# Layer 0's gates: the order of the squares of the weights, and the distance of the adaLN sums

## The chip, the core and the metric

One NeuronCore of a Trainium2 chip runs the whole program. Its engines work side by side: TensorE (PE: matmuls, with the weight loads shown as PEld), VectorE (DVE), ScalarE (ACT), GpSimd (POOL), and SyncE (SP), which here only issues DMAs. Each engine takes its own instructions strictly in order, and waits on semaphores for the others. The metric is the time of one execution on the device in microseconds (us); the kernel before has a median of 1865.01 us in three runs (1864.7 to 1866.88).

## What is computed

A stack of two layers over 1024 latent tokens and 256 context tokens of width 1024. Each layer modulates its input by adaLN, mixes tokens, multiplies with a SiLU gate, projects out and normalises.

```python
def adaln(cvec, w, b):
    m = jax.nn.silu(cvec) @ w + b
    return jnp.split(m, 3, axis=-1)
...
        shift, scale, gate = adaln(c, ada_w[i], ada_b[i])
        shift_c, scale_c, gate_c = adaln(c_ctx, ada_w[i], ada_b[i])
        h = x * (1.0 + scale[:, None, :]) + shift[:, None, :]
        h_c = ctx * (1.0 + scale_c) + shift_c
...
        q_lat, kv_lat, k_pe, gate = jnp.split(t @ w_in, splits, axis=-1)
        q = (rms_norm(q_lat, g_qa) @ w_qb).reshape(bsz, n, A_HEADS, A_NOPE + A_ROPE)
        kv = (rms_norm(kv_lat, g_kva) @ w_kvb).reshape(bsz, n, A_HEADS, A_NOPE + A_V)
```

Layer 0 is multi-head latent attention (the last lines), layer 1 differential attention. This document is about a stretch of layer 0: the columns of `t @ w_in` that make the gate, and what is done beside them.

## The kernel before

**The gates.** For 1280 tokens in 10 tiles of 128 and 1024 gate columns in 4 quarters of 256 there are 40 gate tiles. `gate_tile` (L310) is 24 matmuls in a row (8 slices of the width, three products of high and low halves each), then a SiLU on ScalarE and a store of the result. The first two are done at the end of the stage before; the other 38 in the loop under `with spool("p0g")`. The weights of the next quarter are loaded and split by `gate_w` (L297): ScalarE casts the high half, GpSimd subtracts the low half.

**What runs beside them.** After each of these 38 tiles the loop calls `next(side, None)` once, so the generator `beside_gates` gives 38 stretches of other work. Only TensorE's order is written by hand (`manual_schedule`): its instructions run exactly in the order of the program text, so a matmul that is issued in a stretch stands between two gate tiles. On the other engines and in SP's queue a scheduler puts instructions in an order of its own before the run, by when it takes them to be ready and by their place in the text; after that their order is fixed too. A tile of a tag with a few buffers can be written when an earlier user of that buffer is done.

**The first part of the side work**, `up_weights` (L372), prepares layer 0's up-projection weights and the scales for its half-precision attention. It has a tag `u` with four buffers, through which all loads go. Its items, each followed by a `yield`:

- `q_weight`, four times: load 128 x 768 of w_qb, multiply by a gain on VectorE (L382), cast the high half on ScalarE (L176), subtract the low half on GpSimd (L177).
- `k_weight`, two times: the same for 128 x 512 of w_kv (L291).
- `rope_chunk`, three times: load a chunk of the rotary keys; for the two latent chunks load cosines and sines as well and rotate (`rope`, L277 to L280, with a fourth buffer of `u`); for the context chunk copy.
- `square`, ten times: ScalarE squares a chunk of weights into a tile `wsq` (three buffers); the first two (`sq_v`, L392) load their chunk of the value weights into `u` first, the next two square the k weights, the last six the q weights. Each `square` from the third on also issues the `column_sums` of the square two before: one matmul (L403) into a bank `c`, of which there are two, and VectorE's maximum of it (L407), after which the bank is free.

Then follow the last two column sums, the range of the rotary keys, one small matmul (L448), the scales, and the store of the split keys to `kpf_d` (L459, L460).

**The second part**, `ada_dve` (L463), makes three thirds of adaLN's product, (layer 1 shift), (layer 1 scale) and (layer 0 gate), for the two conditioning vectors s = 0, 1. Per third it loads eight tiles `adw` of 128 x 1024 (three buffers) and sums them on VectorE, weighted by a column `ck`, into `acc[0]` and `acc[1]` (three buffers): L497 begins a sum, L501 adds to it. `finish` then sums over partitions: for a shift or scale 8 matmuls for each vector (L470) and one addition (L473); for the gate two matmuls for each vector (L482), two additions (L483) and a store to `gates_d` (L484). The steps of `finish` are taken, one in a stretch, while the next third is being summed.

Behind the gates come the first projections and loads for layer 0's attention; SP's loads for them (L290, L621, L622, L627) stand behind the last `gates_d` store in its queue.

Of the kernel before, what the change touches and what calls it, by code (L numbers as in the profile page):

```python
# [14 lines left out]
ALU = mybir.AluOpType  # L15
AX = mybir.AxisListType

P = 128
D = 1024
# [34 lines left out]
def hybrid_kernel(  # L54
# [7 lines left out]
    pe, act, dve, pool, sp = nc.tensor, nc.scalar, nc.vector, nc.gpsimd, nc.sync  # L62
# [6 lines left out]
    def nm(s):  # L69
        uid[0] += 1  # L70
        return f"{s}_{uid[0]}"
# [39 lines left out]
    def col(n, name, dt=F32):  # L111
        return cpool.tile([P, n], dt, tag=name, name=name)
# [11 lines left out]
    sc = col(16, "sc")  # L124
# [82 lines left out]
    acc = [hs.tile([P, D], F32, name=f"hacc{s}") for s in range(2)]  # L207
# [12 lines left out]
    for k in range(KT):  # L220
        for g in (1, 0):
            w = hs.tile([P, D], F32, tag="adaw", bufs=6, name=nm("adaw"))
# [149 lines left out]
    def up_weights(pa):  # L372

        u = lambda w=768: pa.tile([P, 768], F32, tag="u", bufs=4, name=nm("u"))[:, :w]
        vm = pa.tile([P, 8], F32, name="vm")
        kr = pa.tile([ROPE, NTOK], F32, name="kr")

        def q_weight(j, hh):
            c = slice(hh * 768, hh * 768 + 768)
            ws = u()  # L380
            sp.dma_start(ws, w_qb[j * P:(j + 1) * P, c])
            dve.tensor_scalar_mul(ws, ws, gqa[:, j:j + 1])  # L382
            split(wqH[:, j, c], wqL[:, j, c], ws, e_lo=pool)

        def k_weight(hh):
            c = slice(hh * 512, hh * 512 + 512)
            kv_weight(c, wkH[:, c], wkL[:, c], u(512))

        def sq_v(dst, c):
            wv = u(512)  # L390
            sp.dma_start(wv, w_kv[:, 1024 + c.start:1024 + c.stop])
            act.activation(dst, wv, AF.Square, scale=gkva)  # L392

        norms = ((0, [sq_v], 1024), (1, [lambda d_, c: act.activation(d_, fv(wkH[:, c]), AF.Square)], 1024),
                 (2, [lambda d_, c, j=j: act.activation(d_, fv(wqH[:, j, c]), AF.Square) for j in range(2)], 1536))
        jobs = [(f, i, c0, j == 0, j == len(parts) - 1) for i, parts, n in norms
                for c0 in range(0, n, 512) for j, f in enumerate(parts)]
        cur = [None]

        def column_sums(sq, i, c0, first, stop):  # L400
            if first:
                cur[0] = bank("c")
            pe.matmul(cur[0], onr, sq, start=first, stop=stop)  # L403
            if stop:
                dst = vm[:, i:i + 1]
                d_ = vm[:, 6:7] if c0 else dst
                dve.tensor_reduce(d_, cur[0], axis=AX.X, op=ALU.max)  # L407
                if c0:
                    dve.tensor_tensor(dst, dst, d_, op=ALU.max)

        def rope_chunk(c0, n):
            c = slice(c0, c0 + n)
            kt = u(512)[:ROPE]
            sp.dma_start(kt[:, :n], kp_d[:, c])
            if c0 < SEQ:
                tabs = [u(512)[:ROPE] for _ in range(2)]
                for j in range(2):
                    sp.dma_start(tabs[j], cs0[j, :ROPE, c])
                rope(kt, n, tabs[0], tabs[1], u(512)[:ROPE], kr[:, c])
            else:  # L420
                dve.tensor_copy(kr[:, c], kt[:, :n])

        wait = []

        def square(f, i, c0, first, stop):
            sq = pa.tile([P, 512], F32R, tag="wsq", bufs=3, name=nm("wsq"))
            f(sq, slice(c0, c0 + 512))
            wait.append((sq, i, c0, first, stop))
            if len(wait) == 3:
                column_sums(*wait.pop(0))  # L430

        sq = [(square, a) for a in jobs]
        rc = [(rope_chunk, a) for a in CHUNKS]
        for f, a in (sq[:2] + [(q_weight, (j, hh)) for j in range(2) for hh in range(2)] + [(k_weight, (hh,)) for hh in range(2)]
                     + [rc[0], sq[2], rc[1], sq[3], rc[2]] + sq[4:]):
            f(*a)
            yield
        for w in wait:
            column_sums(*w)
            yield  # L440
        dve.tensor_reduce(vm[:ROPE, 3:4], kr, axis=AX.X, op=ALU.max, apply_absolute_value=True)
        for i, n in ((0, KVL), (1, KVL), (2, 4 * QL)):
            pool.tensor_scalar(vm[:, i:i + 1], vm[:, i:i + 1], 1.01 * n, 1e-30, op0=ALU.mult, op1=ALU.add)
        pool.tensor_tensor(vm[:, 0:3], vm[:, 0:3], poshalf[:, 0:1].to_broadcast([P, 3]), op=ALU.pow)
        yield
        yield
        bk = bank("c")
        pe.matmul(bk[:, :ROPE], vm[:ROPE, 3:4].to_broadcast([ROPE, P]), idn[:ROPE, :ROPE], start=True, stop=True)  # L448
        dve.tensor_reduce(vm[:, 4:5], bk[:, :ROPE], axis=AX.X, op=ALU.max)
        dve.tensor_tensor(vm[:, 1:2], vm[:, 1:2], vm[:, 4:5], op=ALU.max)  # L450
        p2 = pa.tile([P, 3, 2], F32, name="p2")
        pow2_of(vsc0, usc0, vm[:, 0:1], 8192.0, p2[:, 0, :])
        pow2_of(ksc0, vm[:, 4:5], vm[:, 1:2], 32.0, p2[:, 1, :])
        pow2_of(qsc0, vm[:, 5:6], vm[:, 2:3], 32.0, p2[:, 2, :])
        dve.scalar_tensor_tensor(esc0, vm[:, 4:5], SC0, vm[:, 5:6], op0=ALU.mult, op1=ALU.mult)
        dve.scalar_tensor_tensor(sh0, ksc0, math.log(4.0) / SC0, qsc0, op0=ALU.mult, op1=ALU.mult)
        kh_, kl_ = (u().bitcast(F16)[:ROPE, :NTOK] for _ in range(2))
        split16(kh_, kl_, kr, ksc0[:ROPE, :])
        sp.dma_start(kpf_d[:, 0, :], kh_)  # L459
        sp.dma_start(kpf_d[:, 1, :], kl_)  # L460
        yield

    def ada_dve(tile_, thirds):  # L463

        def finish(layer, g, acc):
            if g < 2:
                cb = bank("c")
                for s, a_ in enumerate(acc):
                    for j in range(KT):
                        pe.matmul(cb[:, 2 * j + s:2 * j + s + 1], a_[:, j * P:(j + 1) * P], ones[:, 0:1],  # L470
                                  start=True, stop=True)
                    yield
                dve.tensor_tensor(cols1[:, g * KT:g * KT + KT, :], cb[:, :16].rearrange("p (a b) -> p a b", b=2),  # L473
                                  adac[:, g * KT:g * KT + KT].rearrange("p (a o) -> p a o", o=1).to_broadcast([P, KT, 2]),
                                  op=ALU.add)
                return
            gr = tile_("adw")[:1, :]
            sp.dma_start(gr, ada_b[layer:layer + 1, g * D:(g + 1) * D])
            for s, a_ in enumerate(acc):
                for c0 in (0, 512):  # L480
                    bk = bank("c")
                    pe.matmul(bk[:1, :512], ones[:, 0:1], a_[:, c0:c0 + 512], start=True, stop=True)  # L482
                    dve.tensor_tensor(a_[:1, c0:c0 + 512], gr[:, c0:c0 + 512], bk[:1, :512], op=ALU.add)  # L483
                sp.dma_start(gates_d[layer, s:s + 1, :], a_[:1, :])  # L484
                yield

        end = iter(())
        for layer, g in thirds:
            acc = []
            for k in range(KT):  # L490
                w = tile_("adw")
                sp.dma_start(w, ada_w[layer, k * P:(k + 1) * P, g * D:(g + 1) * D])
                for s in range(2):
                    ck = sc[:, 2 * k + s:2 * k + s + 1]
                    if k == 0:
                        acc.append(tile_("acc"))
                        dve.tensor_scalar_mul(acc[s], w, ck)  # L497
                        if s == 0:
                            next(end, None)
                    else:  # L500
                        dve.scalar_tensor_tensor(acc[s], w, ck, acc[s], op0=ALU.mult, op1=ALU.add)  # L501
                if k:
                    next(end, None)
                yield
            end = finish(layer, g, acc)
        yield
        for _ in end:
            yield
# [31 lines left out]
    def beside_gates():  # L540
        with spool("p0side") as sp_:
            for i, _ in enumerate(up_weights(sp_)):
                if i % 5 in (1, 4):
                    yield
        with spool("p0side2") as sp_:
            t_ = lambda tag: sp_.tile([P, D], F32, tag=tag, bufs=3, name=nm(tag))
            yield from ada_dve(t_, ((1, 0), (1, 1), (0, 2)))
# [358 lines left out]
    with ow_ctx, spool("o0") as op0:  # L906
# [14 lines left out]
        for t in (8, 9, 0, 1, 2, 3, 4, 5, 6, 7):  # L921
# [5 lines left out]
            s = 0 if t < 8 else 1  # L927
# [574 lines left out]
```

## Time and profile before

| | us |
|---|---|
| median of three runs | 1865.01 |
| the profiled execution | 1863.27 |
| its span (first to last instruction) | 1861.5 |
| TensorE busy in the span | 1688.1 (91%) |
| VectorE, ScalarE, GpSimd busy | 1239.5, 1076.3, 834.9 |
| first gate tile starts, last one ends | 97.4, 244.5 |

A row of a timeline reads: start, duration, engine, line, operation, out<-in, shape, count; in brackets the engine's idle time before it and who ended it. A row of waits reads: engine, what waited, who released it, then total us, times, longest. A row of stretches has the stretch, its length, TensorE's busy time and number of matmuls, the granted share of its clock, the busy share of the DMA engines and what they moved. A row of SP gives the issue of a DMA, not its landing. Rows with a count above one are merged: their duration runs from the first start to the last end.

### The profile page before, as it was taken

The numbers are of one execution on the slowest core, as the hardware profiler recorded it, in microseconds if no ns is written. First come the engines' busy times: TensorE is split into PE (matmuls) and PEld (weight loads), VectorE is DVE, ScalarE is ACT, GpSimd is POOL, SyncE is SP. The second block draws the span as 40 slices with busy tenths as digits, with TensorE's granted clock in tenths as the row PEclk, the third lists the DMA queues.
The fourth block names the chain that finished last, engine by engine and source line by source line (L and its number), as shares of the span: only waits on it lengthen the run. The fifth ranks groups of instructions, "written<-read, shape, count | busy, mean of one in ns | idle before, by whom it ended". The sixth has DMA issues, their size and how long they took to land. (4 is left out here: it accounts for less than half of the span.)

```text
span 1861.5 us, 36543 instructions
## 1 busy us (share of the span) xinstructions
PE 1688.1 (91%) x14468; PEld 1232.8 (66%) x14468; DVE 1239.5 (67%) x2069; ACT 1076.3 (58%) x2143; POOL 834.9 (45%) x741
## 2 busy tenths in 40 slices
PE   7889988999999998969879899999999999988998
PEld 3888965666666565557656575767676666666776
DVE  7547655665565666526764777777877777878674
ACT  3442156877877778811123676676767676767542
POOL 1443026767767776846652213232222222423654
PEclk8998999999999999979989999999999999999999
DMA  8247530111110113153334222222211212223342
GB/s 297 73 119 217 166 107 14 42 32 37 39 45 24 39 43 79 50 172 128 124 118 115 70 66 58 61 65 63 64 50 41 48 48 58 65 52 139 100 132 68
DMA packets 111225, 154.84 MB, mean 83 GB/s; under 512 B 13415, under 2 KB 84679, under 8 KB 111054
## 3 DMA queue, kind: packets, MB, share of 16 engines
q1 hardware_dynamic: 104238, 146.22, 26.5%
q10 hardware_dynamic: 6816, 6.29, 1.0%
q8 instruction: 114, 1.87, 0.4%
q14 instruction: 57, 0.47, 0.1%
HBM read 98.65 MB, written 27.07 MB: 68 GB/s over the span
## 5 line engine op out<-in xcount | busy, mean ns | idle before, releaser
L733 POOL TENSOR_TENSOR pl<-p,ph 128x1024 f16<-128x1024 f32 (+1 forms) x176 | 363.8, 2073 | 152.5 <-ACT ph L732 124.9
L1187 ACT ACTIVATE p<-ps_b,mx 128x512 f32<-128x512 f32 (+1 forms) x384 | 230.3, 617 | 82.0 <-DVE mx L1183 81.8
L731 ACT ACTIVATE p<-ps_a,esc 128x1024 f32<-128x1024 f32 (+1 forms) x176 | 189.0, 1074 | 99.5 <-PE ps_a L789 93.6
L713 DVE TENSOR_REDUCE mx<-ps_a 128x1 f32<-128x1024 f32 x128 | 155.5, 1222 | 135.3 <-PE ps_a L711 135.2
L732 ACT CAST ph<-p 128x1024 f16<-128x1024 f32 (+1 forms) x176 | 177.1, 1006 | 5.5
L1181 DVE TENSOR_REDUCE mx<-ps_b 128x1 f32<-128x512 f32 x256 | 165.5, 681 | 0.0
L802 PE MATMUL ps_d<-Vh,pl 128*128 128x65 f16 x1344 | 147.0, 194 | 6.7 <-POOL pl L733 6.7
L799 PE MATMUL ps_d<-Vh,ph 128*128 128x65 f16 x1344 | 149.1, 195 | 0.0
L801 PE MATMUL ps_d<-Vl,ph 128*128 128x64 f16 x1344 | 147.9, 193 | 0.0
L185 PE MATMUL ps_b<-h1H,wH 128*128 128x512 f16 (+1 forms) x384 | 133.5, 348 | 14.1 <-DVE pl L182 7.1
L185 PE MATMUL ps_b<-wH,h1H 128*128 128x256 f16 x512 | 139.5, 272 | 4.4 <-ACT p L1187 4.1
L1212 POOL TENSOR_TENSOR sm<-sm,us 128x1 f32<-128x1 f32 x64 | 19.5, 305 | 271.2 <-DVE sm L1191 257.9
L187 PE MATMUL ps_b<-wH,h1L 128*128 128x256 f16 x512 | 139.5, 273 | 0.0
L186 PE MATMUL ps_b<-wL,h1H 128*128 128x256 f16 x512 | 139.5, 273 | 0.0
L1164 PE MATMUL ps_b<-KS,QS 128*128 128x512 f16 (+1 forms) x384 | 126.1, 345 | 11.6 <-DVE pl L182 6.1
L799 PEld LDWEIGHTS <-ph 128*128 128x128 f16 x1344 | 123.8, 98 | 18.1 <-issue 4.9
L187 PE MATMUL ps_b<-h1H,wL 128*128 128x512 f16 (+1 forms) x384 | 133.0, 346 | 0.8 <-DVE wL L182 0.8
L186 PE MATMUL ps_b<-h1L,wH 128*128 128x512 f16 (+1 forms) x384 | 133.1, 347 | 0.0
L801 PEld LDWEIGHTS <-ph 128*128 128x128 f16 x1344 | 124.5, 99 | 12.2 <-issue 0.3
L787 PE MATMUL ps_a<-qH,KH 100*128 100x512 f16 x320 | 122.4, 383 | 9.7 <-ACT p L731 4.5
L1165 PE MATMUL ps_b<-KS,Q 128*128 128x512 f16 (+1 forms) x384 | 129.2, 345 | 0.0
L802 PEld LDWEIGHTS <-pl 128*128 128x128 f16 x1344 | 123.7, 98 | 8.3 <-POOL pl L733 8.3
(369 smaller groups left out, 5138.5 us busy)
## 6 DMA issues: line engine op xcount, KB each, us to landing
ws<-in_dw SPq DMA_DIRECT2D x30, 512.0 KB, 3.9
adw<-in_ada_w SPq DMA_DIRECT2D x24, 512.0 KB, 4.4
g<-sg_d SPq DMA_DIRECT2D x18, 512.0 KB, 3.5
adaw<-in_ada_w SPq DMA_DIRECT2D x16, 512.0 KB, 6.8
sg_d<-gg ACTq DMA_DIRECT2D x40, 128.0 KB, 4.7
o<-o_d SPq DMA_DIRECT2D x10, 512.0 KB, 3.6
o_d<-op SPq DMA_DIRECT2D x7, 640.0 KB, 3.7
xt<-in_xT SPq DMA_DIRECT2D x16, 256.0 KB, 3.6
```

What stands on the lines that cost most here:

```text
L185: pe.matmul(ps, aH, bH, start=start, stop=False, skip_group_check=skip)
L186: pe.matmul(ps, aH, bL, start=False, stop=False, skip_group_check=skip)
L187: pe.matmul(ps, aL, bH, start=False, stop=stop, skip_group_check=skip)
L713: dve.tensor_reduce(mx[:, t, 0:1], ps, axis=AX.X, op=ALU.max)
L731: act.activation(p32[:, :n], st, AF.Exp, scale=esc0)
L732: act.copy(ph[:, :n], p32[:, :n])
L733: pool.tensor_tensor(pl[:, :n], p32[:, :n], ph[:, :n], op=ALU.subtract)
L799: pe.matmul(pv[:, t, :], ph[:, ts], Vh[:, k, h, :], start=(k == kcs[0] and t == 0), stop=False, skip_group_check=True)
L801: pe.matmul(pv[:, t, :V0], ph[:, ts], Vl[:, k, h, :], start=False, stop=False, skip_group_check=True)
L802: pe.matmul(pv[:, t, :], pl[:, ts], Vh[:, k, h, :], start=False, stop=(k == NT - 1), skip_group_check=True)
L1181: dve.tensor_reduce(mx[:, 2 + 2 * m + i:3 + 2 * m + i], b, axis=AX.X, op=ALU.max, negate=True)
L1187: act.activation(p[m][:, c0:c0 + n], b, AF.Exp, bias=nb, accum_out=sm[:, 2 + 3 * m + i:3 + 3 * m + i])
```

## The change

Edits in the two generators and in their caller. `CHUNKS` has three entries.

```diff
-        for f, a in (sq[:2] + [(q_weight, (j, hh)) for j in range(2) for hh in range(2)] + [(k_weight, (hh,)) for hh in range(2)]
-                     + [rc[0], sq[2], rc[1], sq[3], rc[2]] + sq[4:]):
+        for f, a in [(q_weight, (j, hh)) for j in range(2) for hh in range(2)] + [(k_weight, (hh,)) for hh in range(2)] + rc + sq:
             f(*a)
             yield
...
+        def add(k, s):
+            ck = sc[:, 2 * k + s:2 * k + s + 1]
+            if k == 0:
+                acc.append(tile_("acc"))
+                dve.tensor_scalar_mul(acc[s], ws[k], ck)
+            else:
+                dve.scalar_tensor_tensor(acc[s], ws[k], ck, acc[s], op0=ALU.mult, op1=ALU.add)
+
         for layer, g in thirds:
-            acc = []
+            acc, ws = [], []
             for k in range(KT):
-                w = tile_("adw")
-                sp.dma_start(w, ada_w[layer, k * P:(k + 1) * P, g * D:(g + 1) * D])
-                for s in range(2):
-                    ck = sc[:, 2 * k + s:2 * k + s + 1]
-                    if k == 0:
-                        acc.append(tile_("acc"))
-                        dve.tensor_scalar_mul(acc[s], w, ck)
-                        if s == 0:
-                            next(end, None)
-                    else:
-                        dve.scalar_tensor_tensor(acc[s], w, ck, acc[s], op0=ALU.mult, op1=ALU.add)
-                if k:
+                ws.append(tile_("adw"))
+                sp.dma_start(ws[k], ada_w[layer, k * P:(k + 1) * P, g * D:(g + 1) * D])
+                if k == 0:
+                    continue
+                if k == 1:
+                    add(0, 0)
+                    add(1, 0)
+                    yield
                     next(end, None)
-                yield
+                    add(0, 1)
+                    add(1, 1)
+                    yield
+                else:
+                    next(end, None)
+                    add(k, 0)
+                    add(k, 1)
+                    yield
             end = finish(layer, g, acc)
...
             for i, _ in enumerate(up_weights(sp_)):
-                if i % 5 in (1, 4):
+                if (i % 2 if i < 12 else i % 3 == 2):
                     yield
```

- The items of `up_weights` now run: four q weights, two k weights, three rotary chunks, ten squares. Before, two squares came first and two stood between the rotary chunks.
- The caller asks for two items in each of the first six stretches and for three in each of the next four; before it asked for two and three in turn. The part fills ten stretches, where it filled nine and a part of the tenth.
- A third of adaLN still fills eight stretches. Its tiles 0 and 1 are loaded in the first of them and summed for vector 0 there, for vector 1 in the second; `finish` of the third before takes its first step in the second stretch (it was the first) and its second in the third. All thirds begin one stretch later, so the first step of `finish` stands two gate tiles later than before, and so does the second; the last third's two steps stand one gate tile later.
- No instruction is added or taken away.

## The prediction

> **What bounds the kernel now.** I read the page first, then the waits of TensorE inside the gates of layer 0 (97 to 245 us), then TensorE's busy time and clock by stretch, then the engines' timelines around the two places found.
>
> ```profile
> span 1861.5 us, 36543 instructions
> ```
> ```profile
> PE ps_c L470 <- DVE acc L501: 4.4, 1, 4.4
> PE ps_c L403 <- DVE vm L407: 3.2, 1, 3.2
> PE ps_c L403 <- ACT wkH L176: 3.0, 1, 3.0
> ```
> ```profile
> core 0: us, PE busy (x), PEclk, DMA share, GB/s
> 121.90:125.80 3.90, 0.52 (x2) 1.00 0.36 98
> 125.80:132.70 6.90, 4.04 (x18) 0.51 0.28 77
> 132.70:167.20 34.50, 34.50 (x281) 1.00 0.65 192
> 167.20:170.20 3.00, 0.12 (x2) 1.00 0.96 265
> 170.20:180.40 10.20, 8.64 (x40) 0.50 0.84 230
> ```
>
> In this stage TensorE is full except at two places, both inside small matmuls that were threaded between gate tiles: column sums of squares (L403) and the last step of an adaLN third (L470). Since TensorE's order is written by hand, whatever is late there stops all gate tiles behind it. Idle time is only part of the price: after each place the clock stands at half.
>
> Place one: idle 3.90 - 0.52 = 3.4 and 6.90 - 4.04 = 2.9, and half of the 4.04 us worked at clock 0.51, 2.0: together **8.3 us**. Place two: 2.9 and 1.6 idle, and half of 8.64, 4.3: **8.8 us**. A full-clock matmul costs 34.5/281 = 0.123 us, so a gate tile of 24 takes 2.9 us.
>
> Why place one is late: both waits are for VectorE in the end.
>
> ```profile
> 114.32 0.62 DVE L382 TENSOR_SCALAR u<-u,gqa 128x768 f32<-128x768 f32 x1 [11.23 <-DMA u<-in_w_qb]
> ...
> 116.35 1.82 DVE L382 TENSOR_SCALAR u<-u,gqa 128x768 f32<-128x768 f32 x1 [0.39 <-DMA u<-in_w_qb]
> ...
> 124.15 0.68 DVE L407 TENSOR_REDUCE vm<-ps_c 128x1 f32<-128x512 f32 x1
> 126.63 0.01 DVE L277 LOAD_MASK_SELECT u<-u  x1 [1.79 <-POOL wkL L177]
> 126.63 0.71 DVE L277 STREAM_SHUFFLE u<-u 32x512 f32<-32x512 f32 x1
> 127.25 0.66 DVE L278 TENSOR_TENSOR kr<-u,u 32x512 f32<-32x512 f32 x1
> 127.84 0.67 DVE L407 TENSOR_REDUCE vm<-ps_c 128x1 f32<-128x512 f32 x1
> ...
> 131.10 0.67 DVE L278 TENSOR_TENSOR kr<-u,u 32x512 f32<-32x512 f32 x1
> ```
>
> The reductions L407, which free the two banks "c", sit in VectorE's queue behind weight scalings and a rotation (L277) that wait for buffers. The third column sum finds its bank at 124.8 instead of 122, the fourth at 128.5.
>
> **The change: squares last.** Item by item, the old order put the first column sum (cs0) after the fourth tile of this loop; the new one asks two items per tile, so cs0 is issued with item 11, in the sixth call: two tiles later.
>
> ```profile
> 115.60 0.39 PE L403 MATMUL ps_c<-wsq,onr 128*128 128x512 f32 x1
> ...
> 171.76 0.58 PE L470 MATMUL ps_c<-ones,acc 128*128 128x1 f32 x2 [4.43 <-DVE acc L501]
> ```
>
> TensorE therefore reaches cs0 at 115.6 + 2 x 2.9 = 121.4. But cs0 needs the square of the first value-weight chunk, and that chunk is loaded into a buffer of the tag u, of which there are four. Before, its load was the first of all:
>
> ```profile
> 107.04 0.91 SPq L391 DMA_DIRECT2D u<-in_w_kv  x2
> 108.00 6.54 SPq L381 DMA_DIRECT2D u<-in_w_qb  x4
> 117.77 2.46 SPq L290 DMA_DIRECT2D u<-in_w_kv  x2
> ```
> ```profile
> 111.07 0.72 ACT L392 ACTIVATE wsq<-u,gkva 128x512 fp32r<-128x512 f32 x1 [3.53 <-DMA u<-in_w_kv]
> ```
> ```profile
> 115.89 8.05 POOL L177 TENSOR_TENSOR wqL<-u,wqH 128x768 fp32r<-128x768 f32 x4 [9.30 <-ACT wqH L176]
> 123.91 2.67 POOL L177 TENSOR_TENSOR wkL<-u,wkH 128x512 fp32r<-128x512 f32 x2
> ```
> ```profile
> DMA to landing us min/median/max: 1.9/3.0/6.8
> ```
> (the last row is that of all loads into u.) Now it is the sixteenth user of u, behind four q weights, two k weights, eight tiles of two rotations and one of a copy. It gets the buffer that held the second rotation's cosines. The chain to it:
>
> - First q weight: issued at 107.0, landed 4.0 later like the first load before (111.07), so 111.1. From VectorE's scaling to GpSimd's subtraction 115.89 - 114.32 = 1.6: GpSimd starts at 112.7 instead of 115.9.
> - GpSimd's six subtractions are back to back, 8.05 + 2.67 = 10.7 long. I add 1.4 for a hole: the second q weight lands about 113, while GpSimd is in its first subtraction, and a scaling in that state took 1.82 us, not 0.62. Then comes its cast, so the second subtraction begins near 115.9, not 114.5. The first rotation's last buffer is free at 124.8, against 126.6 before.
> - From there to the end of the second cosine multiply: 131.77 - 126.63 = 5.1 before, with two reductions in between that are gone; what is left is 1.3 for shuffle and multiply, 2.0 for the reload (the least landing is 1.9) and 1.3 again: 129.4.
> - SP issues the copy's load, 0.4, then the value chunk; 3.0 to land, 0.75 to square: TensorE goes on at **133.6**.
>
> So TensorE stands 133.6 - 121.4 = 12.2 us where it stood 6.3 before. The idle time ends at half clock; I take the 2.0 us that place one cost so far. At the fourth column sum the bank of the second must be reduced first, 0.8 (a 0.67 us reduction and its two handovers; VectorE is free now). The other six sums have a gate tile for each three of them and wait for nothing. New price 15.0, old 8.3: **+6.7 us**. The ten squares and their ten matmuls are the same in number and cost.
>
> Bounds: without the hole -1.4; if loads land as late as 6.8 (row above) the q weights arrive together, without a hole but from 113.8 on, +1.3; the value chunk in 4.0 instead of 3.0, +1.0; half clock for 3.3 us of work instead of 4.0 (second row below), -0.35, or for 8.64 as at place two, +2.3; the bank 0 to 1.2.
>
> ```profile
> 49.90:53.00 3.10, 0.01 (x1) 1.00 0.00 2
> 54.20:57.50 3.30, 3.30 (x11) 0.50 0.10 23
> ```
>
> [...] The row shows a scaling that is slow beside GpSimd, not why. [...]
>
> **adaLN sums.** The first third's sums are now consumed two tiles later on TensorE for one vector and again one tile on for the other (L470 after the tenth and eleventh tile behind the L448 matmul instead of the eighth and ninth). The loads do not move against the work they hang on: the new loop begins one call later, but its DMAs and sums are free of TensorE's order and follow the store of kpf_d, as before.
>
> ```profile
> 152.31 1.42 DVE L497 TENSOR_SCALAR acc<-adw,sc 128x1024 f32<-128x1024 f32 x2 [4.20 <-DMA adw<-in_ada_w]
> 154.87 18.49 DVE L501 SCALAR_TENSOR_TENSOR acc<-adw,sc,acc 128x1024 f32<-128x1024 f32 x14 [1.14 <-DMA adw<-in_ada_w]
> ```
> ```profile
> 168.11 7.65 POOL L177 TENSOR_TENSOR wgL<-wgs,wgH 128x256 fp32r<-128x256 f32 x6 [22.29 <-ACT wgH L176]
> ```
>
> TensorE was 4.4 us early; two tiles are 5.8, so 1.4 to spare and no wait: **-8.8 us**. Against it, a bound: if VectorE keeps the written order, the second sum waits for tile 1 (154.87), and tile 0 is free only after 154.87 + 1.3 + 0.7 = 156.8, not 153.7.
>
> ```profile
> adw<-in_ada_w SPq DMA_DIRECT2D x24, 512.0 KB, 4.4
> ```
>
> Its buffer's next load then lands at 161.2, where the fifth of the 14 sums began at 154.87 + 4 x 1.2 = 159.7: 1.6 late, 0.2 short of the spare time. GpSimd's splits (168.11) stretch the last sums as before. So 0 to 3 us can come back, 0 is nearest. The same 16 sums and 32 L470 matmuls per third remain. Later thirds have their two tiles more as well.
>
> **The end of the stage.** The last gate row is stored one tile later, and SP's loads for the attention queue behind it.
>
> ```profile
> 239.46 0.22 SPq L484 DMA_DIRECT2D gates_d<-acc  x1
> 239.78 0.83 SPq L290 DMA_DIRECT2D p<-in_w_kv  x2
> ```
> ```profile
> 250.38 0.87 DVE L291 TENSOR_SCALAR p<-p,gkva 128x512 f32<-128x512 f32 x2
> ```
>
> They move by a tile, from 239.8 to 242.7; at 3 us to land (the median above), one behind the other, they are there by about 248, and VectorE asks at 250.4: that cover holds. Without it, up to 1 us.
>
> **Sum:** +6.7 - 8.8 + 0 = -2.1 us. The profiled execution took 1863.27 us (span and 1.8 around it), 1.7 less than the median of the runs, 1865.01. So 1861.2 in its terms, **1862.9** for the median. By all bounds at once it is -4.7 to +6.9 us; 0.2% is 3.7 us, and less than that can't be told from no change.
>
> **Rivals.** (1) *The first wait is short*: GpSimd's chain has no hole, half clock lasts 3.3 us, the bank is free in time: -1.4 - 0.35 - 0.8 against my sum, so -4.65, 1860.4. For it: one q scaling at 0.62 us while loads landed 1 us apart. Against: four q loads now share the burst. (2) *It does what it says*, both waits vanish, -17.1 us, 1847.9: needs the value chunk by 121.4, so a buffer of u by about 117.6; the third row of SP shows a buffer of the first q weight free only at 117.8 and the next in line taking it. (3) **Slower:** the sums of the first third still come late at L470, over some 2 us, and the clock halves again there. Price 3 of wait and 4.3 of half clock as at place two: -2.1 + 7.3 = +5.2, 1870.2. It decides from about 2 us of lateness, which takes the written order and one slow load. For it: 3.1 us of idle time at 49.90 were followed by half clock. Against: 1.4 us to spare.
>
> [...]
>
> **How the numbers follow.** Forecast 0.50 (its own range 1861.3 to 1867), rival 1 0.24, rival 2 0.08, rival 3 0.18. Faster is 1 and 2, 0.32; slower is 3. The range 1858.8 to 1869.2 leaves out rival 2 and half of rival 3.
>
> **What would show it.** Right: one wait of about 12 us at L403 for the value chunk (its load issued near 129.8), none over 1 us at another L403, none at L470, the clock at half once instead of twice in the stage, L448 some 6 to 7 us later than 143.7 and the last gate tile ending within 3 us of 244.5. Wrong: cs0 issued near 121, a wait at L470 over 2 us, or first q weight subtracted before 112 or after 114.

## The result, and the profile after

The changed kernel takes 1869.33 us in the median of 17 runs (1864.82 to 1876.58), the kernel before, in 17 runs beside them, 1866.08. The ratio, which is that of the means (1870.42 and 1865.64), is 1.0026, 95% interval 1.0013 to 1.0038: some 4.9 us **slower** (the medians lie 3.25 apart). The forecast was 2.1 us faster; the time and the place of the loss are those of rival 3 (5.2 slower), its cause is not.

The waits of TensorE in the gates of layer 0 in the changed kernel (columns as before: who waits, for whom, total us, times, longest):

```profile
PE ps_c L403 <- ACT wsq L392: 12.1, 1, 12.1
PE ps_c L469 <- DVE acc L494: 3.1, 1, 3.1
PE ps_c L403 <- DVE vm L407: 0.6, 1, 0.6
```

Line numbers are one lower from L447 on: L447 is the old L448, L469 the old L470, L494 adds to a sum as L501 did. One wait is long at L403, as forecast; one is left at L469, which the forecast had at zero. TensorE's busy time and clock in the stretches of the two places:

```profile
core 0: us, PE busy (x) PEld busy (x) DVE busy (x) ACT busy (x) POOL busy (x), PEclk, DMA share, GB/s
119.96:132.30 12.34, 0.22 (x3) 0.06 (x1) 6.88 (x12) 2.50 (x6) 2.34 (x2) 0.65 0.35 104
132.30:137.30 5.00, 5.00 (x22) 4.90 (x23) 0.69 (x1) 1.56 (x3) 0.00 (x0) 0.50 0.00 0
178.70:181.80 3.10, 0.00 (x1) 0.00 (x0) 3.10 (x4) 0.35 (x1) 0.80 (x1) 0.98 0.84 247
181.80:188.50 6.70, 6.67 (x31) 6.67 (x32) 5.36 (x5) 1.50 (x5) 4.62 (x4) 0.50 0.70 237
```

Priced as in the prediction: place one 12.34 - 0.22 = 12.1 idle, half of 5.00, and 0.6 for the bank, 15.2 (forecast 15.0, old 8.3). Place two 3.1 idle and half of 6.67, 6.4 (forecast 0, old 8.8). 15.2 + 6.4 - 17.1 = **+4.5**, and the measured loss is 4.9. The whole loop says the same. Its third tile and the first matmul behind its last tile, in the timelines of the kernel before and of the changed one:

```profile
104.08 0.28 PE L185 MATMUL ps_a<-wgH,hH 128*128 128x256 f32 x1
244.50 0.40 PE L185 MATMUL ps_a<-latH,wkH 128*128 128x512 f32 x1
```
```profile
102.68 0.28 PE L185 MATMUL ps_a<-wgH,hH 128*128 128x256 f32 x1
149.31 0.40 PE L447 MATMUL ps_c<-idr,vm 32*128 32x32 f32 x2
247.92 0.40 PE L185 MATMUL ps_a<-latH,wkH 128*128 128x512 f32 x1
```

From the third tile to the end the loop takes 247.92 - 102.68 = 145.2 us against 140.4: 4.8 more. (This run reached the loop 1.4 us sooner, so times are compared from the third tile, or from L447, on.) The loop accounts for the whole loss: outside it the two profiled executions differ by -1.4 us ahead of the loop and +1.4 behind it. In the tables below this length is called the loop.

**Place one** went by the chain of the prediction, in its order. VectorE's scalings, GpSimd's subtractions, the loads and the squares of the value chunks:

```profile
110.77 2.54 DVE L382 TENSOR_SCALAR u<-u,gqa 128x768 f32<-128x768 f32 x2 [1.20 <-DMA u<-in_w_qb]
```
```profile
110.51 1.85 POOL L177 TENSOR_TENSOR wqL<-u,wqH 128x768 fp32r<-128x768 f32 x1 [5.60 <-ACT wqH L176]
113.73 5.94 POOL L177 TENSOR_TENSOR wqL<-u,wqH 128x768 fp32r<-128x768 f32 x3 [1.36 <-ACT wqH L176]
```
```profile
127.60 0.89 SPq L391 DMA_DIRECT2D u<-in_w_kv  x2
```
```profile
131.47 1.36 ACT L392 ACTIVATE wsq<-u,gkva 128x512 fp32r<-128x512 f32 x2 [8.34 <-DMA u<-in_w_kv]
```

GpSimd's hole is 1.36 us (1.4 in the sum), because the second scaling went beside the first subtraction. The first subtraction began at 110.51, which with the 1.4 us of this run's early start is 111.9 (112.7 in the sum), and the value chunk's load was issued at 127.60, so 129.0 (129.8 in the sum). From its issue to its square it took 3.9 us, where the sum had 3.0. So TensorE went on at 132.24, which is 133.6, just as forecast, because two errors of 0.8 and 0.9 us cancelled: that the end fits so well is luck. The second scaling ran from 110.77 to 112.78, 2.0 us where the one at 108.94, with GpSimd idle, took 0.62, and ended 0.4 us behind the first subtraction; why it is slow beside GpSimd no trace shows.

**Place two** is where the sum failed. What lies between the last column sums and the first adaLN sums, on VectorE, GpSimd and SP's queue (the last as waits) of the changed kernel:

```profile
146.09 0.69 DVE L407 TENSOR_REDUCE vm<-ps_c 128x1 f32<-128x512 f32 x1 [2.64 <-PE ps_c L403]
...
147.56 0.69 DVE L407 TENSOR_REDUCE vm<-ps_c 128x1 f32<-128x512 f32 x1
...
150.38 0.22 DVE L284 TENSOR_SCALAR p<-vm 128x1 int32<-128x1 int32 x2 [1.94 <-POOL vm L443]
...
160.58 1.42 DVE L492 TENSOR_SCALAR acc<-adw,sc 128x1024 f32<-128x1024 f32 x2 [5.21 <-DMA adw<-in_ada_w]
164.03 1.28 DVE L494 SCALAR_TENSOR_TENSOR acc<-adw,sc,acc 128x1024 f32<-128x1024 f32 x1 [2.04 <-DMA adw<-in_ada_w]
```
```profile
148.81 0.74 POOL L177 TENSOR_TENSOR wgL<-wgs,wgH 128x256 fp32r<-128x256 f32 x1
149.50 0.85 POOL L443 TENSOR_TENSOR vm<-vm,poshalf 128x3 f32<-128x3 f32 x1
```
```profile
SPq L500 <- DMA kpf_d<-u: 0.7, 1, 0.7
```

The same step L284 in the kernel before, where L448 stood at 143.69 and the row of tile 1's first sum at 154.87:

```profile
143.06 0.22 DVE L284 TENSOR_SCALAR p<-vm 128x1 int32<-128x1 int32 x2 [1.25 <-POOL vm L444]
```

Against L447 (149.31), L284 comes 1.1 us behind where it was 0.6 ahead, and tile 1's first sum 14.7 behind where it was 11.2. So the loads did move against the work that they hang on. Two candidates show. The norms are late: against the small matmul VectorE's last maximum ends 1.0 us later than before (-0.9 instead of -1.9), and then their power (L443) stands in GpSimd's queue behind a split for the next quarter's weights (0.7 us). And the second adaLN load waited for the landing of the second store of `kpf_d`, which no load did before. Tile 1's first sum is 3.5 us late by this; the other 0.9 us of the lateness arises in the sums themselves, which take 17.7 us from there to the end of the last one for vector 0, against 16.8: four of them, beside GpSimd's splits from 173.74 on, took 1.44 to 1.76 us instead of 1.28, and two before, beside those from 168.11 on (1.75 and 1.74). VectorE took both first sums together (160.58, x2), so the "written order" that rival 3 counted on did not come.

### The profile page after: what moved, and what is told of

Read it like the earlier page. It is cut to its first block, busy times and chain, and to the rows that moved or that the text cites. A ratio compares the mean times of both kernels' runs of the same rounds, so it can differ in the third digit from the quotient of the medians.

```text
span 1866.3 us, 36546 instructions
## 1 busy us (share of the span) xinstructions
PE 1686.0 (90%) x14468; PEld 1229.9 (66%) x14468; DVE 1240.7 (66%) x2069; ACT 1075.8 (58%) x2143; POOL 833.5 (45%) x741
## 5 line engine op out<-in xcount | busy, mean ns | idle before, releaser
L812 PEld LDWEIGHTS <-ph 128*128 128x128 f16 x1344 | 123.9, 98 | 12.1
```

The lines of the kernel that those rows point to most:

```text
L812: pe.matmul(pv[:, t, :V0], ph[:, ts], Vl[:, k, h, :], start=False, stop=False, skip_group_check=True)
```

## The experiments

All ratios are to the kernel before on the same chip; the loop of the kernel before is 140.4 us, that of the changed one 145.2. A loop is that of one profiled execution. e1_ada_only and e11_ada_again are the same kernel, and their loops differ by 2.7 us: in the second, place one waited 1.4 us longer and the clock stood at half for 10.2 us instead of 6.8. So loops less than 3 us apart are not told apart by them alone. The times set against the small matmul further down repeat better: tile 1's first sum comes at +11.3, +11.3 and +11.2 in e1, e11 and e12, and at +14.7, +14.6 and +14.8 in the changed kernel, e2 and e4.

| | median us | ratio, 95% interval | loop us |
|---|---|---|---|
| changed kernel | 1869.33 | 1.0026, 1.0013 to 1.0038 | 145.2 |
| e1_ada_only | 1856.42 | 0.9949, 0.9937 to 0.9962 | 130.5 |
| e11_ada_again | 1855.36 | 0.9950, 0.9932 to 0.9967 | 133.2 |
| e2_squares_only | 1872.85 | 1.0043, 1.0029 to 1.0056 | 146.5 |
| e3_values_first | 1862.34 | 0.9982, 0.9973 to 0.9992 | 137.6 |
| e4_finish_later | 1864.66 | 0.9990, 0.9980 to 1.0000 | 140.1 |
| e5_layout | 1866.04 | 1.0004, 0.9988 to 1.0020 | 141.8 |
| e6_sums_sooner | 1864.28 | 0.9998, 0.9987 to 1.0008 | 139.3 |
| e7_layout_sooner | 1863.02 | 0.9987, 0.9976 to 0.9998 | 139.2 |
| e8_spread | 1861.91 | 0.9982, 0.9968 to 0.9995 | 136.2 |
| e9_sums_ahead | 1856.27 | 0.9948, 0.9927 to 0.9969 | 129.9 |
| e10_sums_ahead_x | 1854.62 | 0.9944, 0.9927 to 0.9961 | 129.0 |
| e12_narrow_twice | 1873.83, one run | | 147.3 |

### The two parts alone

**e1_ada_only**, against the changed kernel:

```diff
-        for f, a in [(q_weight, (j, hh)) for j in range(2) for hh in range(2)] + [(k_weight, (hh,)) for hh in range(2)] + rc + sq:
+        for f, a in (sq[:2] + [(q_weight, (j, hh)) for j in range(2) for hh in range(2)] + [(k_weight, (hh,)) for hh in range(2)]
+                     + [rc[0], sq[2], rc[1], sq[3], rc[2]] + sq[4:]):
...
-                if (i % 2 if i < 12 else i % 3 == 2):
+                if i % 5 in (1, 4) or i == 23:
```

> The order and pacing of the squares are those of the kernel before (with one more stretch so that adaLN begins in the same stretch as in the changed kernel); only the adaLN part of the change is in. Theory (the late sums at L469 come from place one's new order, not from the adaLN part): the waits at L403 are those of before, 3.2 and 3.0 us; the first sum follows the L447 matmul by about 8.6 us as before, the last s=0 sum by 28, TensorE asks at 29, so no wait over 1 us at the last step of the first third and no half clock there. That gives back the 8.6 us of before: about 1857.5. Rival (the adaLN part itself makes the sums late, by its written order or its loads): sums still 11 us behind L447, a wait of 3 us and half clock at the last step, about 1863 to 1866.

Its waits of TensorE up to the end of the gates, and the last step of the first third on its timeline:

```profile
PE ps_c L403 <- DVE vm L407: 2.9, 1, 2.9
PE ps_c L403 <- ACT wkH L176: 2.2, 1, 2.2
```
```profile
172.70 1.84 PE L470 MATMUL ps_c<-ones,acc 128*128 128x1 f32 x16
```

Place one waits for the same as in the kernel before, 5.1 us instead of 6.2; nothing waits at L470, 29.2 us behind L448 (143.47). Measured 9.5 us faster (0.9949). The adaLN part is worth what the prediction gave it, so its step failed only together with the other part. **e11_ada_again** is the same kernel once more:

> e1_ada_only once more, on the same chip as the two others. Theory (the adaLN part alone is worth its 8.6 us): 8 to 11 us less than the kernel before, no wait at the last step of a third. Rival (its first measurement was luck of the chip): under 5 us.

The ratio is 0.9950, 9.3 us faster, with no wait at L470: not luck.

**e2_squares_only**, against the kernel before: the new order and pacing, the old `ada_dve`.

> Only the order and pacing of the squares are changed; adaLN is that of the kernel before. Theory: one wait of about 12 us at L403 as in the changed kernel, +7 us; L470 is reached two tiles (5.8 us) sooner behind L447 than in the changed kernel, while the sums are as late as there (last s=0 sum 32.5 us behind L447), so a wait of 6 to 9 us and half clock behind it, 2 to 4 us more than before: 1874 to 1877. Rival (the sums are late only because the adaLN part starts them later): the sums keep their 28 us behind L447, the wait is 4.4 us as before, about 1873.

The waits were 11.8 at L403 and 5.2 at the last step of the third, where the sum ended 31.7 us behind L447. Measured 1.0043, 8.0 us slower, 1 us under the range: TensorE came to that step one tile sooner than in the changed kernel (at +26.5 instead of +29.4), not two, since the new pacing has a stretch more. The time, 1872.85, is the one that the rival had named; what decides is the sum, which ended at 31.7 and not at 28, and tile 1's first sum at +14.6. The squares alone make the sums late.

### Place one: more than the load

**e3_values_first**, against the changed kernel:

```diff
-        for f, a in [(q_weight, (j, hh)) for j in range(2) for hh in range(2)] + [(k_weight, (hh,)) for hh in range(2)] + rc + sq:
+        for f, a in (sq[:2] + [(q_weight, (j, hh)) for j in range(2) for hh in range(2)] + [(k_weight, (hh,)) for hh in range(2)]
+                     + rc + sq[2:]):
```

> The changed kernel, but the two value chunks are loaded and squared first of all, as before; all else stays in the new order, so the first column sum stands where the change puts it. Theory (place one's wait is the value chunk's load behind the four buffers u): the 12 us wait at L403 and the half clock behind it vanish, and no other wait at L403 is over 1 us, -14 us at place one; the wait of 3 us at L469 stays or grows by up to 3, since its sums hang on the rotation and the norms and not on TensorE: 1854 to 1859. Rival (the order makes TensorE wait for banks, norms or weights in any case): waits of 5 us or more at L403 or at L447 take its place, 1863 to 1869.

Its waits, and VectorE around them:

```profile
PE ps_c L403 <- DVE vm L407: 8.7, 2, 7.0
PE ps_c L470 <- DVE acc L495: 1.0, 1, 1.0
```
```profile
131.70 0.71 DVE L277 STREAM_SHUFFLE u<-u 32x512 f32<-32x512 f32 x1
132.32 0.66 DVE L407 TENSOR_REDUCE vm<-ps_c 128x1 f32<-128x512 f32 x1
```

The 12 us for the value chunk are gone, but 8.7 for banks stand in their place: the first column sum is made at 122.7 and reduced at 132.3, behind the whole first rotation and the first step of the second. Theory and rival both hold in part, and the time, 1862.34, lies nearer to the rival's. The load is what TensorE waits for last in the changed kernel; were it early, VectorE's rotations, late by the same four buffers, would hold TensorE nearly as long. Measured 3.4 us faster than the kernel before (0.9982). Not all of that is place one: at L470 the wait is 1.0 us with 3.4 us at half clock behind it, 2.7 us where the changed kernel pays 6.4, because here too a square is the first item (see e5_layout).

### Place two: what makes the sums late

**e4_finish_later**, against the changed kernel, has one call less of the last step, so the steps of `finish` come one tile later:

```diff
                     add(1, 0)
                     yield
-                    next(end, None)
                     add(0, 1)
```

> The changed kernel, but the last step of each adaLN third is put one more tile behind. Theory (3.1 us of lateness at L469 and the half clock behind them are what is left of place two): TensorE asks at 32.1 us behind L447 for a sum that ends at 32.5, the wait falls to about 0.4 us, the clock does not halve there, 6 us come back: about 1863. [...] Rival (the sums' lateness moves along with the step, or the end of the stage loses what is won): 1869.

The wait fell to 0.3 us, but the half clock behind it only from 6.8 to 3.4 us, which costs 1.7; the time, 1864.66, lies about that much over the theory's 1863 (see the last section).

**e5_layout**, against the changed kernel:

```diff
         wait = []
+        wsq = lambda: pa.tile([P, 512], F32R, tag="wsq", bufs=3, name=nm("wsq"))
+        first_wsq = [wsq()]
...
-            sq = pa.tile([P, 512], F32R, tag="wsq", bufs=3, name=nm("wsq"))
+            sq = first_wsq.pop() if first_wsq else wsq()
```

> The changed kernel, but the buffers wsq are laid out ahead of the buffers u, as in the kernel before (there a square was the first item, so wsq was the first of the two to be asked for). Nothing else differs. In the changed kernel the second adaLN load waited for the landing of the second store of kpf_d, and the first sum of tile 1 came 14.7 us behind L447; in e3_values_first, where a square is again the first item, no such wait was seen and it came at 12.6. Theory (two thirds of the wait at L469 are this load, because its buffer now covers one of u): no wait for kpf_d, tile 1 at 12.6 behind L447, the wait at L469 falls from 3.1 to 1.0 us, the half clock behind it from 3.2 us lost to 1.7: about 1865.5. Rival (the norms alone make the sums late, the load's wait is covered by the sums of tile 0): wait 3.1 as in the changed kernel, 1869.

**e6_sums_sooner**, against the changed kernel, and **e7_layout_sooner**, both edits:

```diff
-                if (i % 2 if i < 12 else i % 3 == 2):
+                if (i % 2 if i < 12 else i in (14, 20, 21, 23)):
```

> The changed kernel, but the last three column sums go one stretch sooner, so that six stand in one stretch and none in the stretch ahead of L447, whose own stretch stays. Theory (one third of the wait at L469 is the norms: three reductions in the stretch right ahead of L447 push the power on GpSimd behind the splits of the next quarter): VectorE's L284 comes ahead of L447 as in the kernel before, not 1.1 us behind it; the first sum follows L447 by about 9.5 us instead of 11.3, the wait at L469 is 1.5 instead of 3.1, and the six sums in one stretch cost about 1 us in bank waits: 1867 to 1868.5. Rival (the norms were not late because of the threes): L284 stays behind L447 and the wait at 3.1: 1869 to 1870.

> Both of the two edits, the layout and the sooner sums. Theory (these two causes are all of the lateness): the last s=0 sum ends about 28.8 us behind L447 and TensorE asks at 29.2, so neither a wait nor half clock at L469; 6.4 us come back less the 1 us of bank waits: about 1864. Rival (a third cause remains): a wait of 1 us or more at L469 with half clock behind it, 1866 to 1868.

VectorE's rows of e5 (the first fence), e6 and e7, for L284 and tile 1's first sums:

```profile
151.31 0.22 DVE L284 TENSOR_SCALAR p<-vm 128x1 int32<-128x1 int32 x2 [1.93 <-POOL vm L445]
...
163.08 3.67 DVE L496 SCALAR_TENSOR_TENSOR acc<-adw,sc,acc 128x1024 f32<-128x1024 f32 x3
```
```profile
150.23 0.21 DVE L284 TENSOR_SCALAR p<-vm 128x1 int32<-128x1 int32 x2 [2.62 <-POOL vm L443]
...
164.99 2.48 DVE L494 SCALAR_TENSOR_TENSOR acc<-adw,sc,acc 128x1024 f32<-128x1024 f32 x2 [2.61 <-DMA adw<-in_ada_w]
```
```profile
150.44 0.21 DVE L284 TENSOR_SCALAR p<-vm 128x1 int32<-128x1 int32 x2 [2.62 <-POOL vm L445]
...
163.82 2.47 DVE L496 SCALAR_TENSOR_TENSOR acc<-adw,sc,acc 128x1024 f32<-128x1024 f32 x2
```

Set against the small matmul (L447 or its equal) of each timeline, in us:

| | small matmul at | L284 | tile 1's first sum | TensorE asks | goes on | wait |
|---|---|---|---|---|---|---|
| before | 143.69 | -0.6 | +11.2 | +23.6 | +28.1 | 4.4 |
| e1_ada_only | 143.47 | -0.6 | +11.3 | +29.2 | +29.2 | none |
| changed | 149.31 | +1.1 | +14.7 | +29.4 | +32.5 | 3.1 |
| e5_layout | 150.24 | +1.1 | +12.8 | +29.4 | +30.9 | 1.5 |
| e6_sums_sooner | 152.03 | -1.8 | +13.0 | +29.4 | +30.1 | 0.7 |
| e7_layout_sooner | 152.23 | -1.8 | +11.6 | +29.2 | +29.2 | none |

The layout alone brings tile 1's sum 1.9 us forward, the sooner norms alone 1.7, both together 3.1; with both, no wait and no half clock are left at place two, and the changed kernel comes down from 4.9 us slower to 2.4 faster (0.9987). That is 7.3, where 6.4 was the price of place two. e5 came near its theory (1866.04 for about 1865.5, a wait of 1.5 us for 1.0). e6 came out better than expected, 1864.28 under its range, because the clock did not halve behind its 0.7 us. So these two causes make the lateness, up to the 0.4 us by which tile 1 in e7 is still behind the kernel before; the sums themselves again take 16.8 us there.

Two things are not separated. e6 moves the last three column sums and, with them, the norms' own place in the text one stretch sooner, so it does not say which of the two counts. And the wait for `kpf_d` shows in SP's queue in the changed kernel, e2, e4 and e6, and in none in which a `wsq` is asked for ahead of the first `u`; but it is 0.7 us long, and the layout is worth 1.9: the load also landed 6.2 us after its issue in the changed kernel and 4.8 in e5 (5.8 in the kernel before). What makes that difference stays open.

### Looking for a better kernel

**e8_spread** is e1_ada_only with the stretches ending at i in (1, 4, 6, 8, 9, 11, 12, 14, 20, 23).

> e1_ada_only with another pacing of the same items in the same number of stretches: the first two column sums one tile later, the third and fourth two tiles later, the last six in one stretch, L448 in the stretch where it was. Theory (place one's price in the old order is only that TensorE comes before the k weights' square and before VectorE's reductions behind the rotations, and two tiles of 2.9 us cover it): no wait over 1 us at the third and fourth column sum, bank waits of up to 2.5 us among the last six, no or a short half clock: 4 to 7 us less than e1_ada_only, 1849 to 1853. Rival (the reductions move along with the sums in VectorE's queue, so the wait only changes its place): waits of 5 us or more at L403 in all, 1855 to 1858.

Neither came: 1861.91 (0.9982) is over both ranges. The waits were 3.3 us at L403 and 1.9 at L470, the latter with half clock behind it: with six column sums in the last stretch ahead of L448 (142.04), L284 came 2.8 us behind it. It is the lateness of the norms once more, with the old order of the squares.

**e9_sums_ahead** and **e10_sums_ahead_x**, against e1_ada_only (e10 has one stretch more, which ends at 22; e9 also has e4's edit):

```diff
-                     + [rc[0], sq[2], rc[1], sq[3], rc[2]] + sq[4:]):
+                     + sq[2:4] + rc[:1] + sq[4:8] + rc[1:] + sq[8:]):
...
-                if i % 5 in (1, 4) or i == 23:
+                if i in (1, 4, 6, 8, 9, 10, 12, 17, 20, 23):
```

> From e1_ada_only: the reductions of the first five bank fills stand ahead of the rotations in VectorE's order (first rotation behind the second square of the k weights' turn, second rotation and copy behind the sixth column sum), the third and fourth column sum stand one tile later, the last three in the stretch ahead of L448, and the last step of each adaLN third one tile later. Theory (place one's price is VectorE's reductions behind rotations that wait for buffers u, and the k weights' square): no wait over 1 us at L403, no half clock there, 6 to 8 us less than e1_ada_only at place one; the maximum of the rotated keys is now the last thing ahead of L448, which may wait up to 2.5 us: 1849 to 1854. Rival (the rotations' chain sets the time of L448 in any order): what is won at L403 is lost at L448 in a wait of 4 us or more with half clock, 1855 to 1859.

> As e9_sums_ahead, but L448 one stretch later, with adaLN and the end of the stage behind it, and the last step of an adaLN third where e1_ada_only has it. Theory of e9: neither L403 nor L448 waits, but the last gate rows are stored a tile later, behind the last gate tile, and up to 3 us of the gain are lost at the end of the stage: 1850 to 1854. Rival: as for e9, 1855 to 1859.

Both took what e1_ada_only takes (0.9948 and 0.9944 against 0.9950 for e11_ada_again, on the same chip), so the gain of 6 to 8 us did not come, and neither did the rival's wait at L448. The longest wait at L403 became one for ScalarE's squares, 2.7 and 3.2 us; for VectorE 1.8 us are left in e9 and 0.6 in e10. Whether place one can be had for nothing stays open. The kernel to keep is e1_ada_only: the adaLN part with the old order of the squares, 0.5% faster than the kernel before and 0.8% faster than the changed one (0.9949 / 1.0026 = 0.9923).

### The clock behind small matmuls

**e12_narrow_twice**, against e1_ada_only, in `finish`:

```diff
-                    for j in range(KT):
+                    for j in sorted(2 * list(range(KT))):
```

> e1_ada_only with each of the 16 one-column matmuls at L470 issued twice, the second over the result of the first, so a set takes 3.4 us instead of 1.7 and no engine has to be waited for. In e4_finish_later a wait of 0.26 us and the 16 matmuls behind it were followed by 3.4 us at half clock, in e1_ada_only the 16 alone were not. Theory (such matmuls count nearly as idle for the clock, and a period with about 2 us of idle time and of them is enough): half clock behind most of the four sets, 4 x 1.7 longer for the matmuls and up to 4 x 1.7 more for the clock: 1866 to 1870. Rival (only time without a matmul counts): full clock behind all four sets, 1863.

Two of its four sets (their matmuls start from 172.43 to 175.92 and from 205.60 to 210.38), in stretches that follow the steps of the clock, with the columns of the table of stretches above:

```profile
173.56:176.97 3.41, 3.41 (x32) 3.41 (x32) 0.87 (x2) 1.10 (x3) 1.85 (x4) 1.00 0.86 248
176.97:180.38 3.41, 3.41 (x19) 3.41 (x18) 3.31 (x3) 0.40 (x1) 3.34 (x2) 0.50 0.82 296
...
204.28:207.69 3.41, 3.41 (x33) 3.41 (x31) 0.00 (x0) 0.38 (x1) 0.00 (x0) 1.00 0.20 68
207.69:211.10 3.41, 3.41 (x17) 3.41 (x18) 0.54 (x1) 0.00 (x0) 0.00 (x0) 0.50 0.00 0
211.10:214.51 3.41, 3.41 (x18) 3.41 (x17) 2.78 (x3) 0.00 (x0) 0.00 (x0) 0.50 0.61 167
```

By the profile, whose matmul ends are modelled, TensorE is busy for the whole of each stretch and waits for nothing, and yet the clock is at half behind every set. The loop is 16.9 us longer than in e1_ada_only. The theory holds; the time, 1873.83 in a single run, is over its range: behind two of the sets the clock stood at half for two periods, 20.5 us in all, which costs 10.2 us where the range had up to 6.8.

## Why the prediction was wrong

- **What bounds the kernel**: right. Only the two places moved; the loop's 4.8 us are the whole loss. One reading was too sure: the view puts the first wait of place one down to ScalarE's cast, which ended at 124.89, and the bank came free from VectorE at 124.83, so it can't be said that this wait was for VectorE alone.
- **Place one, +6.7**: right, +6.9 by the same terms (15.2 - 8.3), and the chain in its order: hole 1.4, one wait of 12.1 for the value chunk, one bank wait. The half clock cost 2.5 where the sum had 2.0, and within the chain the weights came 0.8 us sooner and the value chunk 0.9 us slower than the sum had them, which cancelled by luck.
- **Place two, -8.8**: here it failed, at the step "The loads do not move against the work they hang on", and so "1.4 to spare and no wait". I had taken the 28 us between L448 and the last sum from the kernel before as fixed, although the same change reorders everything that stands between them. The gain was 2.4 instead of 8.8. e1_ada_only shows the step right with the old squares, e7_layout_sooner shows both causes of its failure: the new pacing of the last column sums and norms, which brings the norms' scales 1.7 us later against the small matmul, and the first item's tag, which decides where the buffers `u` lie and so what an adaLN load must wait for. The sums' own 0.9 us of stretching, which the prediction took "as before", came with these two and went with them. That the new tiles lie over `u` is concluded from the wait and from its going away in e5; addresses are not in the trace.
- **Rival 3** named the right place and price (3 + 4.3 against the measured 3.1 + 3.3) but another cause: not the written order on VectorE, and not a slow load (6.2 us from issue to landing against 5.8) but a late one, issued 8.5 us behind the small matmul instead of 5.3. Its chance of 0.18 was too small for a margin of 1.4 us across a reordered chain.
- **The end of the stage, 0**: right; TensorE's stall there stayed as it was.
- **What would show it**: the single long wait at L403 and the value chunk's load near 129.8 came; the "none at L470", the "clock at half once" and the last gate tile within 3 us of 244.5 (3.4 later) did not. The wait of 3.1 us at L469 was a sign of being wrong that the prediction had named. So was a first subtraction ahead of 112; it came at 110.51, or 111.9 with the early start, without harm to the forecast for place one.

One thing stayed open: the first adaLN load took 1.2 to 1.4 us to issue in the changed kernel, e2, e3, e4 and e5, where the norms are late by the same 1.7 us, and 0.4 before and in e1, e6 and e7.

## What to carry to other kernels

A distance between two points of the old trace may be used for the new kernel only if nothing between them is reordered; here 28 us became 32.5 because the last column sums and norms were paced otherwise and a pool was laid out differently. When the first item of a generator changes, ask which tag is now allocated first, and whose buffers the next pool's first loads will cover. And try the parts of a change alone: one was worth 9.5 us, the other cost 8.0, and together they cost 4.9, not the -1.5 of their sum.

## What was not expected of the hardware

In e4_finish_later and e12_narrow_twice half clock came without a long idle time ahead of it. In the first 0.26 us of waiting and 16 one-column matmuls were followed by 3.41 us of it (the first fence); in e1_ada_only the 16 alone were not (the second):

```profile
181.33:184.74 3.41, 3.15 (x27) 2.94 (x27) 3.35 (x4) 1.26 (x4) 2.84 (x2) 1.00 0.90 282
184.74:188.15 3.41, 3.41 (x18) 3.41 (x18) 2.84 (x3) 0.86 (x3) 2.65 (x3) 0.50 0.60 193
```
```profile
172.85:176.26 3.41, 3.41 (x32) 3.41 (x31) 2.58 (x4) 0.69 (x2) 3.19 (x3) 1.00 0.89 255
176.26:179.68 3.42, 3.42 (x32) 3.42 (x31) 3.13 (x4) 1.17 (x3) 2.76 (x2) 1.00 0.89 316
179.68:183.09 3.41, 3.41 (x30) 3.41 (x30) 3.41 (x4) 0.38 (x1) 0.00 (x0) 1.00 0.67 191
```

In the traces of the kernel before and the changed one the steps of the clock lie a multiple of 3.41 us apart: half clock at the two places lasted 6.83 and 10.24 us before, and 13.65, most of it waiting, and 6.83 in the changed kernel. A period is a stretch of 3.41 us between such steps. One that holds 1.7 or 1.8 us of one-column matmuls (e1_ada_only) was not followed by half clock; one that holds 0.26 of waiting and the 16 of them was, and so was one that holds 2.1 us of them or more (e12_narrow_twice). So in these runs they counted for the clock like idle time, or nearly. In the traces of the kernel before and the changed one, between 100 and 262 us, the 73 full-clock periods with at most 1.85 us of idle time and one-column matmuls together were followed by full clock, the 6 with 2.65 us or more by half clock. Of the 13 half-clock periods the 6 that held at most 0.45 us of such time were followed by full clock, the 7 with 1.70 us or more by another at half clock. That made a small miss dear: in the changed kernel 3.1 us of waiting were followed by 6.7 us of work at half clock, 3.3 us lost.
